# Modulation chunks of the second layer computed on VectorE instead of TensorE, in a four-layer transformer block on one Trainium2 core

## The chip, the cores and the metric

The kernel is one program on one core of a Trainium2 chip. The core has five instruction queues that matter here: TensorE (PE, with its weight loads shown as PEld), VectorE (DVE), ScalarE (ACT), GpSimd (POOL) and SyncE (SP), which issues the large loads from HBM. Every queue runs its instructions in the order in which they stand, and waits on semaphores for the others. The metric is device time of one execution in microseconds, the median over several runs.

## The reference, cut to what matters

The model has two "first" layers (a mixer and a convolutional feed-forward each) and then two more blocks. There are 256 context tokens and 256 latent tokens of width 1024. Each first layer has six modulation vectors per stream, which scale, shift and gate the activations:

```python
for l in range(DEPTH):                                   # DEPTH = 2
    mod_l = jnp.split((jax.nn.silu(c) @ ada_w[l] + ada_b[l])[:, None, :], 6, axis=-1)
    mod_c = jnp.split((jax.nn.silu(c_ctx) @ ada_w[l] + ada_b[l])[None, None, :], 6, axis=-1)
    hl = modulate(x_lat, norm_g[l, 0], mod_l[0], mod_l[1])    # rms_norm(x, g) * (1 + scale) + shift
    ...
    x_lat = x_lat + mod_l[2] * (mix_l @ w_out[l])
    x_lat = x_lat + mod_l[5] * conv_ffn(modulate(x_lat, norm_g[l, 1], mod_l[3], mod_l[4]), ...)
```

`ada_w[l]` is 1024 by 6144 in float32 (24 MB a layer), and it is multiplied by only two vectors, `silu(c)` and `silu(c_ctx)`. The feed-forward is `(silu(gate) * val) @ w_down`, where gate and val come from `h @ w_up` (1024 by 5632) through a depthwise convolution of width 3.

## The kernel before, in words

**Split products.** Activations and weights are float32. Each is split into a high part (rounded to the matmul's type) and a low part (the rest), and a product is three matmuls: high·high, high·low, low·high (`mm_t`, L438 to L445). A weight tile of 1 MB is loaded into a buffer `raw` (L390), ScalarE writes the high half (`whi`, L400) and the low half is a subtraction: on VectorE (`wlo`, L404), or on GpSimd (L402) where `pool_lo` says so. `pool_lo` is 0 except in the second feed-forward, where it is 2 (every second half). One weight tile is split as two halves of 128x1024, so it has two `whi` and two `wlo`. There are two `raw` buffers, and split halves for three to four tiles.

**The plan.** `_plan` (L126 to L228) writes down the order of all weight tiles. Modulation chunks ("ada", 256 columns of `ada_w` each, 24 a layer) are spread between them, one behind a weight tile. `w()` (L417) hands the next weight tile to a matmul stage, loads and splits one tile ahead, and on its way runs `ada()` (L535 to L560) for each chunk that it meets: 8 small products of 32 stationary columns (each shows as two matmuls in the trace, L538), a copy to SBUF (L541), two transposes (L545) and two or three VectorE instructions of 4 columns (L547 to L553). Layer 0's chunks come early; of layer 1's 24, 16 stand in the first feed-forward, one at its end, six around the second mixer and one in the second feed-forward.

**The first feed-forward** (`_ffn` with l = 0, L1267 to L1353; about 340 to 727 us of the span) runs on all 512 tokens. It goes through the hidden width in six parts (`FPARTS`): up(0), up(1), down(0), up(2), down(1), and so on; an up part has 4 weight tiles (gate and val by turns; the last part 2), a down part 2. An up tile gives two PSUM tiles of 128x512. ScalarE starts the convolution of each from PSUM (L1285), VectorE adds the two other taps from PSUM (L1288, L1289); for a val tile VectorE then multiplies by the gate (L1298, L1299) and makes a low half of the result (L645 in `hilo`). A down tile gives four PSUM tiles, each added to the residual `xt` by two VectorE instructions (L1330). PSUM tiles rotate over five banks (three tagged g, two tagged s) while `K.wide` is set. The second feed-forward runs on the 256 latent tokens alone.

**What sets the order.** The program is recorded in the order in which the Python code runs, and a scheduler then lays each engine's queue from it, with its own estimates. `_Pipe.tick` (L274) is called after every PSUM tile with the number of columns multiplied, and paces work that is interleaved with the matmuls.

Of the kernel before, what the change touches and what calls it, by code (L numbers as in the profile page):

```python
# [10 lines left out]
F32 = mybir.dt.float32  # L11
F32R = mybir.dt.float32r
BF16 = mybir.dt.bfloat16
AF = mybir.ActivationFunctionType
ALU = mybir.AluOpType
# [11 lines left out]
FPARTS = ((0, 4), (4, 4), (8, 4), (12, 4), (16, 4), (20, 2))  # L27

C_ADAB = 0
C_NG = C_ADAB + 96  # L30
# [33 lines left out]
T_MB0 = 5440  # L64
T_MB1 = 5568
T_N = 5824

PERM = [16 * c + 4 * b + a for a in range(4) for b in range(4) for c in range(16)]

# [56 lines left out]
def _plan():  # L126
    p = []
# [7 lines left out]
    def adas(l, js):  # L135
        return [(l, j, c) for j in js for c in range(4)]
# [24 lines left out]
    def spread(extra, start, tail=0, skip=0):  # L161
        q = list(extra)
        body = p[start:]
        del p[start:]
        for i, x in enumerate(body):
            p.append(x)
            if i >= skip and len(q) > tail:
                ada(*q.pop(0))
        while q:
            ada(*q.pop(0))  # L170
# [9 lines left out]
    n = len(p)  # L180
# [3 lines left out]
    n = len(p)  # L184
# [4 lines left out]
    a3, a5 = adas(0, (3,)), adas(0, (5,))  # L189
    spread(a3 + a5[:2], n, 1)  # L190
    n = len(p)
    late = adas(1, (2, 4, 3, 5))
    ffn(0)
    spread(a5[2:] + adas(1, (1, 0)) + late[:9], n, 1)
    o = ("odd_w_in", 0)
    n = len(p)
    for c0 in (512, 0, 256, 1280, 768, 1792, 1536, 1024, 2048):
        cols(o, c0, at=W_N)
    wout(1, 0)
    wout(1, 1)  # L200
    spread(late[9:16 - 1], n, 1, 3)
    n = len(p)
    ffn(1)
    spread(late[16 - 1:], n)
    a = ("a_w_in_2", 0)
    for hg in range(4):
        for g in range(3):
# [29 lines left out]
class _Pipe:  # L237
    def __init__(self):
        self.pending, self.live = [], []
        self.pace = 1e9  # L240
        self.credit = 0.0
        self.later = []

    def defer(self, cost, fn):
        self.later.append([cost, fn])
# [26 lines left out]
            self.live.append(u)  # L272

    def tick(self, cost):  # L274
        if not self.pending and not self.live:
            return
        self.credit += cost
        if self.credit >= self.pace:
            self.credit = min(self.credit - self.pace, self.pace)
            self.slot()  # L280
# [29 lines left out]
class _K:  # L310
# [221 lines left out]
    def ada(self, kind, raw, now=False):  # L532
        nc = self.nc
        _, l, j, c = kind
        acc = self.po(128, 256) if now else self.pg(128, 256)  # L535
        for k in range(KD):
            g = 32 * (k % 4)
            nc.tensor.matmul(acc[g:g + 32], self.sc[:, k, :], raw[:, k], start=(k < 4), stop=(k >= 4))  # L538
        self.pipe.tick(2048)
        sb = self.e(256)  # L540
        nc.scalar.copy(sb, acc)  # L541
        def fin():
            tp = self.pt(128, 2, 128)
            for q in range(2):
                nc.tensor.transpose(tp[:, q], sb[:, 128 * q:128 * q + 128], self.ident)  # L545
            red = self.small([128, 2, 2], "adr")
            nc.vector.tensor_reduce(red, tp.rearrange("p q (g m) -> p q m g", g=4)[:, :, 0:2, :], axis=AX.X, op=ALU.add)  # L547
            o = self.mod[l][:, j, :, 2 * c:2 * c + 2].rearrange("p t q -> p q t")
            a0 = C_ADAB + 48 * l + 8 * j + 2 * c
            nc.vector.tensor_tensor(o, red, self.cols[:, a0:a0 + 2].unsqueeze(2).to_broadcast([128, 2, 2]), op=ALU.add)  # L550
            if j in (1, 4):
                g = C_NG + 16 * l + 8 * (j // 3) + 2 * c
                nc.vector.scalar_tensor_tensor(o, o, 1.0, self.cols[:, g:g + 2].unsqueeze(2).to_broadcast([128, 2, 2]),  # L553
                                               op0=ALU.add, op1=ALU.mult)

        if now:
            fin()
        else:
            self.pipe.defer(6000, fin)

    def stat(self, n):
        return [self.sa.tile([128, n], F32, tag=f"st{n}", name=self.nm("st")), n, 0]
# [704 lines left out]
def _ffn(K, l, segs, st, nxt=None):  # L1267
    nc, tc, cols = K.nc, K.tc, K.cols
    t0, n = segs[0][0], segs[-1][1] - segs[0][0]
    ns = n // 256  # L1270
    with tc.tile_pool(name=f"f{l}", bufs=1, reuse_waits="tile") as pool, tc.tile_pool(name=f"fw{l}", bufs=3, reuse_waits="tile") as wx:
# [30 lines left out]
        def up(i):  # L1302
            f0, fn = FPARTS[i]
            G = pool.tile([128, 2, 4, n], F32R, tag="G", name=K.nm("G"), bufs=2)
            parts[i] = (G[:, 0], G[:, 1])
            for s in range(fn // 2):
                gates = {}

                def eg(m, g):
                    f = f0 + 2 * s + m  # L1310
                    gates[m] = conv(g, cw[:, 0, f:f + 1], cw[:, 1, f:f + 1], cw[:, 2, f:f + 1], cb[:, f:f + 1])

                def ev(m, g):
                    f = f0 + 2 * s + m
                    val = conv(g, hw[:, 0, f:f + 1], hw[:, 1, f:f + 1], hw[:, 2, f:f + 1], hw[:, 3, f:f + 1])
                    glu(f, G[:, 0], G[:, 1], 2 * s + m, gates[m], val)

                first = ((256, 512), (0, 256)) if split and i == 0 and s == 0 else None
                K.gemm_t(K.w(), H, n, eg, 0, first)
                K.gemm_t(K.w(), H, n, ev)  # L1320
# [17 lines left out]
                         K.norm(st[0], l + 1, 0, segs[1], 256, 3) if st else ())  # L1338

        K.wide = True  # L1340
        for i in range(len(FPARTS)):
            up(i)
            if i:
                down(i - 1)
        K.lookahead = 0
        K.wide = False
        nst = nxt(segs) if nxt else None
# [596 lines left out]
def _layout(i):  # L1944
# [28 lines left out]
            w[n, :, 1024 * x:1024 * x + 1024] = src.reshape(ka, 128, cb).transpose(1, 0, 2).reshape(128, 1024)  # L1973
    out["w"] = w
    out["tab"] = _tables()
    return out


# [15 lines left out]
```

## Time and profile before

| what | value |
|---|---|
| median of 3 runs | 1645.6 us (1642.94 to 1646.18) |
| the profiled execution, its own time | 1649.18 us |
| its span, first to last instruction | 1647.4 us |
| mean granted TensorE clock | 0.983 |
| PE busy | 1571.7 us, 95% of the span, 11390 instructions |
| PEld busy | 1378.6 us, 84% |
| DVE busy | 1118.4 us, 68%, 2168 instructions |
| ACT busy | 778.2 us, 47% |
| POOL busy | 265.2 us, 16% |
| HBM read | 228.79 MB, 140 GB/s over the span |

Shares are means over stages of different kinds; the stretch of the first feed-forward has to be read by itself. A busy PE is not PE at its peak, since matmuls overlap: the pitch from one start to the next is what counts. On VectorE an instruction also overlaps the next by a little, so again the start-to-start time is the price.

### The profile page before, as it was taken

The page shows a single profiled execution, that of the slowest core. Times are in us where ns is not written, and L with a number is a line of the kernel's source. Part 1 is how long each engine was busy: PE and PEld are TensorE (multiplying, and loading weights), DVE is VectorE, ACT ScalarE, POOL GpSimd, SP SyncE. Part 2 cuts the span into 40 slices and gives each one's busy share as a digit, 9 for nine tenths or more (in the row PEclk, how much of TensorE's full clock was granted, in tenths as well). Part 3 has the DMA queues.
Part 4 walks back from the last instruction along what each step waited for, and adds up shares of the span by engine and source line. Part 5 has one row for each costly group of instructions (what it writes and reads, how often), then busy time and mean ns, then how long its engine had stood idle before and what let it go on. Part 6 is the DMA issues. An engine that isn't in the chain of part 4 may idle for free.

```text
span 1647.4 us, 28309 instructions
## 1 busy us (share of the span) xinstructions
PE 1571.7 (95%) x11390; PEld 1378.6 (84%) x11390; DVE 1118.4 (68%) x2168; ACT 778.2 (47%) x1427; POOL 265.2 (16%) x239
## 2 busy tenths in 40 slices
PE   5999979999999999999999989999999999999998
PEld 3787857777777788888888889999989999989888
DVE  4676546675645666577677688677675767678897
ACT  3445464354323334334555555554555555555554
POOL 2221100030000000014231344441010101020111
PEclk9989989999999999998999999999999999999999
DMA  8232243334454532331333355554524343516232
GB/s 356 91 112 94 85 150 103 128 144 163 157 185 169 177 130 102 103 108 52 115 116 129 140 199 188 191 186 151 190 98 163 105 174 105 177 59 219 103 118 88
DMA packets 45107, 231.74 MB, mean 141 GB/s; under 512 B 12740, under 2 KB 15940, under 8 KB 18224
## 3 DMA queue, kind: packets, MB, share of 16 engines
q1 hardware_dynamic: 43776, 227.76, 39.9%
q10 hardware_dynamic: 1200, 2.17, 0.4%
q8 instruction: 90, 1.47, 0.4%
q14 instruction: 41, 0.34, 0.1%
HBM read 228.79 MB, written 1.12 MB: 140 GB/s over the span
## 4 chain that ended last, share of the span: by engine, by line
PE 75%; DVE 9%; ACT 4%; DMA 4%; POOL 3%; issue 2%; POOLq 0%; ACTq 0%; DVEq 0%; SPq 0%
PE g L443 10%; PE g L444 10%; PE g L445 9%; PE g L488 6%; PE g L490 6%; PE g L489 6%; PE s L443 4%; PE s L445 4%; PE s L444 4%; DMA raw<-in_w_dram 3%; DVE wlo L404 3%; PE o L1045 3%; PE t L1035 2%; PE g L538 2%; ACT whi L400 1%
## 5 line engine op out<-in xcount | busy, mean ns | idle before, releaser
L404 DVE TENSOR_TENSOR wlo<-raw,whi 128x1024 fp32r<-128x1024 f32 x289 | 358.5, 1252 | 185.8 <-ACT whi L400 185.2
L400 ACT CAST whi<-raw 128x1024 fp32r<-128x1024 f32 x322 | 332.7, 1048 | 315.2 <-DMA raw<-in_w_dram 122.9
L488 PE MATMUL g<-whi,H 128*128 128x256 f32 x1040 | 301.6, 290 | 5.5 <-ACT H L641 2.9
L490 PE MATMUL g<-whi,H 128*128 128x256 f32 x1040 | 297.3, 286 | 1.8 <-DVE H L636 1.0
L489 PE MATMUL g<-wlo,H 128*128 128x256 f32 x1040 | 296.0, 285 | 0.0
L443 PE MATMUL g<-H,whi 128*128 128x256 f32 (+1 forms) x872 | 274.5, 319 | 5.9 <-ACT H L1642 2.9
L444 PE MATMUL g<-H,whi 128*128 128x256 f32 (+1 forms) x872 | 273.7, 315 | 0.9 <-DVE H L636 0.3
L445 PE MATMUL g<-H,wlo 128*128 128x256 f32 (+1 forms) x872 | 271.7, 313 | 0.0
L488 PEld LDWEIGHTS g<-whi,H 128*128 128x128 f32 x1040 | 200.4, 193 | 13.0 <-issue 4.6
L490 PEld LDWEIGHTS g<-whi,H 128*128 128x128 f32 x1040 | 199.8, 192 | 4.0 <-DVE H L636 2.2
L489 PEld LDWEIGHTS g<-wlo,H 128*128 128x128 f32 x1040 | 200.3, 193 | 0.6 <-issue 0.2
L443 PEld LDWEIGHTS g<-H,whi 128*128 128x128 f32 x872 | 164.5, 190 | 22.4 <-ACT H L1642 3.5
L444 PEld LDWEIGHTS g<-H,whi 128*128 128x128 f32 x872 | 165.7, 190 | 13.7 <-DVE H L636 1.9
L445 PEld LDWEIGHTS g<-H,wlo 128*128 128x128 f32 x872 | 165.6, 190 | 9.5
L1009 POOL TENSOR_SCALAR P<-P,rc 128x512 f32<-128x512 f32 (+2 forms) x64 | 55.2, 863 | 491.3 <-DVE rc L1804 258.8
L402 POOL TENSOR_TENSOR wlo<-raw,whi 128x1024 fp32r<-128x1024 f32 x33 | 81.3, 2463 | 105.1 <-ACT whi L400 100.4
L445 PE MATMUL s<-H,wlo 128*128 128x256 f32 (+1 forms) x264 | 88.2, 334 | 1.9 <-DVE wlo L404 1.9
L443 PE MATMUL s<-H,whi 128*128 128x256 f32 (+1 forms) x264 | 89.2, 338 | 0.0
L444 PE MATMUL s<-H,whi 128*128 128x256 f32 (+1 forms) x264 | 87.9, 333 | 0.0
L443 PE MATMUL g<-G,whi 128*128 128x256 f32 (+1 forms) x240 | 79.2, 330 | 2.1 <-DVE e L1289 2.1
L445 PE MATMUL g<-G,wlo 128*128 128x256 f32 (+1 forms) x240 | 78.3, 326 | 0.0
L444 PE MATMUL g<-G,whi 128*128 128x256 f32 (+1 forms) x240 | 78.2, 326 | 0.0
(419 smaller groups left out, 3042.1 us busy)
## 6 DMA issues: line engine op xcount, KB each, us to landing
raw<-in_w_dram SPq DMA_DIRECT2D x209, 1024.0 KB, 4.9
xt<-in_xt_dram SPq DMA_DIRECT2D x4, 512.0 KB, 5.2
mrow<-Md ACTq DMA_DIRECT2D x8, 256.0 KB, 4.6
nab<-in_rpb_dram SPq DMA_DIRECT2D x16, 128.0 KB, 3.6
out_dram<-xt SPq DMA_DIRECT2D x4, 256.0 KB, 4.6
agw<-in_agw_dram SPq DMA_DIRECT2D x1, 512.0 KB, 13.5
mka<-in_tab_dram SPq DMA_DIRECT2D x1, 512.0 KB, 3.4
plr<-in_p_dram SPq DMA_DIRECT2D x2, 256.0 KB, 3.6
```

The source lines that it names most:

```text
L400: nc.scalar.copy(hi, raw)
L402: nc.gpsimd.tensor_tensor(lo, raw, hi.bitcast(F32), op=ALU.subtract)
L404: nc.vector.tensor_sub(lo, raw, hi.bitcast(F32))
L443: nc.tensor.matmul(out, hi[:, k, s], X[0][:, x], start=f, stop=False)
L444: nc.tensor.matmul(out, hi[:, k, s], X[1][:, x], start=False, stop=False)
L445: nc.tensor.matmul(out, lo[:, k, s], X[0][:, x], start=False, stop=l)
L488: nc.tensor.matmul(out, X[0][:, a + k, s], hi[:, k], start=f, stop=False)
L489: nc.tensor.matmul(out, X[0][:, a + k, s], lo[:, k], start=False, stop=False)
L490: nc.tensor.matmul(out, X[1][:, a + k, s], hi[:, k], start=False, stop=l)
L538: nc.tensor.matmul(acc[g:g + 32], self.sc[:, k, :], raw[:, k], start=(k < 4), stop=(k >= 4))
L1009: nc.gpsimd.tensor_scalar(P[1], P[1], rc[:, 1:2], 0.0, op0=ALU.mult, op1=ALU.add)
L1045: nc.tensor.matmul(o[64 * e:64 * e + 64], vv(e, b), u["T"][e][:, b], start=(b == 0), stop=(b == kb - 1))
```

## The change

Layer 1's 24 modulation chunks leave the plan and TensorE. A new generator `vector_ada` loads the same columns, transposed, as 48 tiles `ar` of 128x1024 (an input `v`, 512 KB each, three buffers), and loads both conditioning vectors to all partitions once (`cb`, 1 MB). VectorE then makes, for each of the 48 tiles and the two vectors, one multiply-and-sum over 1024 elements that starts from the bias and writes one column of `mod[1]`: 96 instructions, each with a read of its accumulator behind it. The first of a pair writes its products to a scratch tile `prod`, the second into `ar` itself. The generator is advanced by `tick`, one product per 8600 columns multiplied, during the first feed-forward only. In that stage `pool_lo` becomes 1 for the parts 1 to 4: GpSimd makes all low weight halves of 24 tiles, 48 subtractions that VectorE made before.

```diff
+VECTOR = [(1, j, c) for j in (1, 0, 2, 4, 3, 5) for c in range(4)]
+VPACE = 8600
...
-    late = adas(1, (2, 4, 3, 5))
     ffn(0)
-    spread(a5[2:] + adas(1, (1, 0)) + late[:9], n, 1)
+    spread(a5[2:], n)
...
-    spread(late[9:16 - 1], n, 1, 3)
-    n = len(p)
     ffn(1)
-    spread(late[16 - 1:], n)
...
     def tick(self, cost):
+        if self.side:
+            self.side(cost)
...
+    def vector_ada(self, pool):
+
+        nc = self.nc
+        cb = pool.tile([128, 2, 1024], F32, name="cb")
+        nc.sync.dma_start(cb.rearrange("p t k -> p (t k)"), self.aps["cb"].partition_broadcast(128))
+        jobs = [(l, j, 2 * c + q, n, q) for n, (l, j, c) in enumerate(VECTOR) for q in range(2)]
+
+        def fetch(i):
+            t = pool.tile([128, 1024], F32, tag="ar", name=self.nm("ar"), bufs=3)
+            nc.sync.dma_start(t, self.aps["v"][jobs[i][3]][:, 1024 * jobs[i][4]:1024 * jobs[i][4] + 1024])
+            return t
+
+        tiles = [fetch(0), fetch(1)]
+        yield
+        for t in range(2):
+            for s in (slice(0, 512), slice(512, 1024)):
+                sg = self.e(512)
+                nc.scalar.activation(sg, cb[:, t, s], AF.Tanh, scale=0.5)
+                nc.vector.tensor_scalar(sg, sg, 0.5, 0.5, op0=ALU.mult, op1=ALU.add)
+                nc.vector.tensor_mul(cb[:, t, s], cb[:, t, s], sg)
+            yield
+        for i, (l, j, m, _, _) in enumerate(jobs):
+            raw = tiles.pop(0)
+            if i + 2 < len(jobs):
+                tiles.append(fetch(i + 2))
+            a0 = C_ADAB + 48 * l + 8 * j + m
+            out = self.mod[l][:, j, :, m:m + 1]
+            for t in range(2):
+                prod = raw if t else pool.tile([128, 1024], F32, tag="prod", name=self.nm("prod"), bufs=1)
+                nc.vector.tensor_tensor_reduce(prod, raw, cb[:, t], 1.0, self.cols[:, a0:a0 + 1], ALU.mult, ALU.add,
+                                               out[:, t])
+                if t and j in (1, 4):
+                    g = C_NG + 16 * l + 8 * (j // 3) + m
+                    nc.vector.tensor_scalar(out, out, 1.0, self.cols[:, g:g + 1], op0=ALU.add, op1=ALU.mult)
+                yield
+
+    def side_step(self, steps):
+        state = [0.0]
+
+        def step(cost):
+            state[0] += cost
+            if state[0] >= VPACE:
+                state[0] -= VPACE
+                next(steps, None)
+
+        return step
...
         K.wide = True
+        steps = None
+        if split:
+            steps = K.vector_ada(pool)
+            next(steps)
+            K.pipe.side = K.side_step(steps)
         for i in range(len(FPARTS)):
+            if split:
+                K.pool_lo = int(0 < i < len(FPARTS) - 1)
             up(i)
             if i:
                 down(i - 1)
+        K.pipe.side = None
+        for _ in steps or ():
+            pass
```

**VectorE's queue, from the second weight tile of down(0) to the first tap of up(2).** In the rows, `xt_87` with L1330 (L1379 after the change) is the residual add, `adr` and `mod1` the tail of a modulation chunk, `wlo` a low weight half, and e with L1288 (L1337 after) the first tap. Before:

```order
L1330 SCALAR_TENSOR_TENSOR xt_87<-g_808_4426,mod0_105,xt_87 128x256
L547 TENSOR_REDUCE adr_810_4442<-t_809_4439 128x4
L1330 SCALAR_TENSOR_TENSOR xt_87<-g_811_4447,mod0_105,xt_87 128x256 x2
L404 TENSOR_TENSOR wlo_817_4496<-raw_815_4493,whi_816_4495 128x1024
L404 TENSOR_TENSOR wlo_819_4500<-raw_815_4493,whi_818_4499 128x1024
L1330 SCALAR_TENSOR_TENSOR xt_87<-g_812_4462,mod0_105,xt_87 128x256 x2
L1330 SCALAR_TENSOR_TENSOR xt_87<-s_813_4477,mod0_105,xt_87 128x256 x2
L547 TENSOR_REDUCE adr_826_4533<-t_825_4530 128x4
L404 TENSOR_TENSOR wlo_831_4583<-raw_829_4580,whi_830_4582 128x1024
L404 TENSOR_TENSOR wlo_833_4587<-raw_829_4580,whi_832_4586 128x1024
L1288 SCALAR_TENSOR_TENSOR e_827_4560<-g_823_4516,cols_85,e_827_4560 128x2x255
```

After, from the third PSUM tile of the same weight tile on (behind each product stands the read of its accumulator, left out here):

```order
L1379 SCALAR_TENSOR_TENSOR xt_87<-g_813_4427,mod0_105,xt_87 128x256 x2
L592 ISA ar_853_4695,mod1_106<-ar_853_4695,cb_3543,cols_85 128x1024
L1379 SCALAR_TENSOR_TENSOR xt_87<-g_814_4443,mod0_105,xt_87 128x256 x2
L592 ISA prod_880_4862,mod1_106<-ar_862_4736,cb_3543,cols_85 128x1024
L592 ISA ar_862_4736,mod1_106<-ar_862_4736,cb_3543,cols_85 128x1024
L592 ISA prod_890_4922,mod1_106<-ar_874_4810,cb_3543,cols_85 128x1024
L592 ISA ar_874_4810,mod1_106<-ar_874_4810,cb_3543,cols_85 128x1024
L592 ISA prod_901_4979,mod1_106<-ar_879_4860,cb_3543,cols_85 128x1024
L592 ISA ar_879_4860,mod1_106<-ar_879_4860,cb_3543,cols_85 128x1024
L592 ISA prod_905_5016,mod1_106<-ar_889_4920,cb_3543,cols_85 128x1024
L1337 SCALAR_TENSOR_TENSOR e_825_4512<-g_823_4473,cols_85,e_825_4512 128x2x255
```

The low halves have gone from this queue, and products stand in their place, seven in a row ahead of the first tap of up(2). They are not evenly laid: all 96 stand between up(0) and the last tile of up(3), 81 of them from the first tap of up(1) to there, and 31 in the six weight tiles of up(2) and down(1).

**SP's queue around the same place.** Each row is a load that SP issues; `raw` is a weight tile of 1 MB, or a modulation chunk of the same size. Before:

```order
L390 DMA raw_800_4403<-in_w_dram 128x2048
L390 DMA raw_807_4424<-in_w_dram 128x2048
L390 DMA raw_815_4493<-in_w_dram 128x2048
L390 DMA raw_822_4514<-in_w_dram 128x2048
L390 DMA raw_829_4580<-in_w_dram 128x2048
```

After:

```order
L392 DMA raw_829_4536<-in_w_dram 128x2048
L572 DMA ar_836_4573<-in_v_dram 128x1024
L572 DMA ar_849_4646<-in_v_dram 128x1024
L392 DMA raw_842_4622<-in_w_dram 128x2048
L572 DMA ar_853_4695<-in_v_dram 128x1024
L572 DMA ar_862_4736<-in_v_dram 128x1024
L392 DMA raw_855_4699<-in_w_dram 128x2048
L572 DMA ar_874_4810<-in_v_dram 128x1024
L572 DMA ar_879_4860<-in_v_dram 128x1024
L572 DMA ar_889_4920<-in_v_dram 128x1024
L572 DMA ar_900_4977<-in_v_dram 128x1024
L392 DMA raw_868_4785<-in_w_dram 128x2048
```

Between two weight tiles now stand two to four loads of `ar`, each of which waits until VectorE is through with the `ar` tile three earlier; a weight tile's load waits until GpSimd has made the low halves of the tile two earlier.

## Rows read from the trace of the kernel before

**Rows 1.** Busy us (count) by stretch: PE, PEld, DVE, ACT, POOL; clock; DMA share; GB/s
```profile
355.00:727.00 372.00, 371.98 (x1872) 296.61 (x1871) 227.73 (x361) 132.67 (x182) 0.28 (x1) 1.00 0.41 141
...
640.00:680.00 40.00, 40.00 (x178) 33.10 (x178) 24.57 (x37) 12.35 (x15) 0.00 (x0) 1.00 0.31 105
```
**Rows 2.** Timeline of PE around one chunk: start, us, engine, line, operation, tiles
```profile
403.43 0.39 PE L445 MATMUL s<-H,wlo 128*128 128x512 f32 x1
403.75 1.07 PE L538 MATMUL g<-raw,sc 128*32 128x256 f32 x16
404.75 0.50 PE L443 MATMUL g<-H,whi 128*128 128x512 f32 x1
...
407.41 0.39 PE L445 MATMUL g<-H,wlo 128*128 128x512 f32 x1
407.65 0.38 PE L545 MATMUL t<-ident,e 128*128 128x128 f32 x2
407.78 0.48 PE L443 MATMUL g<-H,whi 128*128 128x512 f32 x1
```
**Rows 3.** Busy time by stretch of line L538 alone: PE, PEld, clock
```profile
355.00:727.00 372.00, 18.20 (x272) 7.09 (x272) 1.00 0.41 141
727.00:925.00 198.00, 8.11 (x113) 3.05 (x113) 0.96 0.33 111
```
**Rows 4.** Timeline of PE where the second mixer begins
```profile
735.34 0.58 PE L488 MATMUL g<-whi,H 128*128 128x256 f32 x1 [2.58 <-ACT H L634]
```
**Rows 5.** Timeline of VectorE in the first feed-forward
```profile
599.22 0.88 DVE L1330 SCALAR_TENSOR_TENSOR xt<-g,mod,xt 128x256 f32<-128x256 f32 x2 [1.45 <-PE g L445]
...
630.61 0.68 DVE L1298 SCALAR_TENSOR_TENSOR e<-e,e 128x512 f32<-128x512 f32 x1
631.21 0.74 DVE L1289 SCALAR_TENSOR_TENSOR e<-g,hw,e 128x510 f32<-128x510 f32 x1
...
632.71 1.23 DVE L404 TENSOR_TENSOR wlo<-raw,whi 128x1024 fp32r<-128x1024 f32 x1
633.86 0.74 DVE L1288 SCALAR_TENSOR_TENSOR e<-s,hw,e 128x510 f32<-128x510 f32 x1
```
**Rows 6.** Timeline of VectorE in the third block: an operation with a sum
```profile
1199.18 0.69 DVE L1801 CUSTOM_DVE_ANT_0 e<-s,mka 128x512 f32<-128x512 f32 x1
...
1199.79 0.69 DVE L1664 TENSOR_TENSOR e<-g,ptcq 128x512 f32<-128x512 f32 x1
```
**Rows 7.** Groups in 1000 to 1110 us, second feed-forward: count, busy us, mean ns
```profile
L402 POOL TENSOR_TENSOR wlo<-raw,whi 128x1024 fp32r<-128x1024 f32 x20 | 48.9, 2447 | 63.2 <-ACT whi L400 58.5 <-PE s L444 4.7
...
L404 DVE TENSOR_TENSOR wlo<-raw,whi 128x1024 fp32r<-128x1024 f32 x20 | 26.2, 1311 | 23.4 <-ACT whi L400 23.4
L645 DVE TENSOR_TENSOR G<-e,G 128x256 fp32r<-128x256 f32 x12 | 13.8, 1148 | 0.0
```
**Rows 8.** Timelines of GpSimd and VectorE in the second feed-forward
```profile
1009.61 2.42 POOL L402 TENSOR_TENSOR wlo<-raw,whi 128x1024 fp32r<-128x1024 f32 x1 [3.24 <-ACT whi L400]
...
1010.02 0.48 DVE L1288 SCALAR_TENSOR_TENSOR e<-s,hw,e 128x255 f32<-128x255 f32 x1 [0.53 <-ACT e L1285]
1010.42 1.89 DVE L645 TENSOR_TENSOR G<-e,G 128x256 fp32r<-128x256 f32 x1
...
1014.55 0.42 DVE L645 TENSOR_TENSOR G<-e,G 128x256 fp32r<-128x256 f32 x1
```
**Rows 9.** Timelines of GpSimd and VectorE in the second mixer
```profile
860.31 1.94 POOL L1009 TENSOR_SCALAR P<-P,rc 128x512 f32<-128x512 f32 x1 [0.58 <-DVE rc L996]
...
867.53 0.69 POOL L1009 TENSOR_SCALAR P<-P,rc 128x512 f32<-128x512 f32 x1 [5.28 <-DVE qms L920]
...
860.15 0.49 DVE L1008 TENSOR_SCALAR P<-P,rc 128x512 f32<-128x512 f32 x1
860.55 1.22 DVE L404 TENSOR_TENSOR wlo<-raw,whi 128x1024 fp32r<-128x1024 f32 x1
```
**Rows 10.** Loads: operation, count, KB each, median us from issue to landing
```profile
raw<-in_w_dram SPq DMA_DIRECT2D x209, 1024.0 KB, 4.9
```

More of the change, by code (lines that the diff above doesn't have):

```diff
@@ L242, in __init__ @@
         self.later = []
+        self.side = None
     def defer(self, cost, fn):
@@ L1975, in _layout @@
     out["tab"] = _tables()
+    out["cb"] = np.concatenate([i["c"][0], i["c_ctx"]])
+    out["v"] = np.stack([i["ada_w"][l][:, 1024 * j + 256 * c:1024 * j + 256 * c + 256].T.reshape(2, 128, 1024)
+                         .transpose(1, 0, 2).reshape(128, 2048) for l, j, c in VECTOR])
     return out
```

## The prediction, made before the run

> **What bounds the kernel now.** I read the busy time by stretch first. In the first feed-forward TensorE is busy for 371.98 of 372 us, VectorE for 227.73, ScalarE for 132.67, and GpSimd does nothing [rows 1]. So TensorE sets the time there, and whatever leaves its queue leaves the stage, as long as nobody else becomes later than it. The second line of the group is the same stage without modulation chunks: 178 matmuls in 40 us, a pitch of 0.225 us, so a weight tile of 48 matmuls takes 10.8 us. That is the clock against which the other engines have to be held.
>
> Then the timeline around one chunk [rows 2]. From the last matmul before it to the first after it are 404.75 - 403.43 = 1.32 us instead of 0.225, and around its two transposes 407.78 - 407.41 = 0.37. A chunk costs TensorE 1.10 + 0.15 = 1.25 us; the matmuls just behind each of the two are a little late too, so I take 1.35.
>
> **What the change removes.** Line L538 alone shows 272 matmuls between 355 and 727 us, 17 chunks of 16 matmuls, and 7 chunks between 727 and 925 us [rows 3]. The plan says that one of the 17 is layer 0's and stays, and that an eighth chunk of layer 1 follows after 925 us. In the first feed-forward 16 chunks go: 16 x 1.35 = 22 us, all of it on the path, since TensorE has no gap there. Behind it 8 go, at most 8 x 1.35 = 11 us. The first of them stands where TensorE waits 2.58 us for the normalised input anyway [rows 4], and the last at the same place of the second feed-forward; I count the other six: 8 us. TensorE's saving is 30 us. The copies, transposes' consumers and 24 loads that go with the chunks lie beside it and count as nothing.
>
> **What it adds to VectorE.** The trace has no product over 1024 elements with a sum. Its two nearest rows: a subtraction of 1024 elements starts 1.15 us before the next instruction [rows 5], and the operation with a sum over 512 elements starts 0.61 us before the next, the read of its accumulator included [rows 6]; a second 512 elements cost the difference between 1.15 and 0.60 (632.71 to 633.86 against 630.61 to 631.21 [rows 5]). Both ways give 1.15 to 1.16 us; 96 products are 110 us. The 48 low halves that go to GpSimd take 48 x 1.15 = 55 us off VectorE. Spread over the whole stage this would fit (228 + 110 - 55 = 283 of some 350 us), but the new order does not spread it. So I make the sum where the products stand thickest, the 18 weight tiles of up(1) to down(2): TensorE needs 18 x 10.8 = 194 us. VectorE has there:
> - 81 products, 81 x 1.15 = 93 us;
> - 48 convolution taps of 0.74 = 35.5 us;
> - 36 gate, val and low-half operations of 0.60 = 21.5 us;
> - 48 residual adds of 0.44 (two in 0.88) = 21 us [rows 5].
>
> Together 171 us, 88% of TensorE's 194. Alone that would hold.
>
> **What GpSimd's halves do to it.** The second feed-forward already has GpSimd halves, 2.45 us each (48.9 us for 20), and there VectorE's operations on two SBUF tiles are long: 1148 ns for an L645 of 256 columns, 1311 for L404 [rows 7]. The timeline shows how: GpSimd's half runs from 1009.61 to 1012.03; the tap that reads PSUM at 1010.02 takes its usual 0.48; the L645 at 1010.42, two SBUF inputs, ends at 1012.31 after 1.89, where it takes 0.42 elsewhere [rows 8]. It stood still until GpSimd was done. The product reads `ar` and `cb`, both in SBUF. No row shows whether it is held like L645; being of the same kind of operands, I take it that it is. The Trainium skill, SBUF — State Buffer, section Who interferes with whom, says the same as a rule: a VectorE instruction with two SBUF inputs contends with a GpSimd instruction that reads SBUF, and the later one waits for the whole of the other. By it the sum is the one below; by a product that is not held it would be the first rival. The trace agrees for the two forms shown, and no run here shows the product.
>
> What a half costs VectorE has two ends. In 1000 to 1110 us the surplus is 12 x (1.15 - 0.42) + 20 x (1.31 - 1.23) = 10.4 us for 20 halves, 0.5 us each [rows 7, 8]; there VectorE had idle time for a half to fall into. The other end is the whole 2.45 us. It cannot choose its moment freely either: where a GpSimd operation (0.69 us when free) came at 860.31, it lost to VectorE's 860.15 and, straight behind it, to the L404 at 860.55, and ended at 862.25 [rows 9]. So in a row of products a half waits, and starts where VectorE turns to an operation that reads PSUM. Such runs last about 0.9 us here: the taps and adds of six tiles (16 x 0.74 + 16 x 0.44 = 19 us) fall into some 20 runs by the order. What is left of 2.45 us, 1.5, is VectorE standing still. With VectorE at 88% by itself this is nearer to the case than 0.5.
>
> 36 halves belong to the 18 tiles: 36 x 1.5 = 54 us, and VectorE needs 171 + 54 = 225 us for TensorE's 194. Five PSUM tiles let TensorE run ahead of the evacuation by about one weight tile, 10 us, which is not lost, since VectorE has no products after down(2) and can catch up there. TensorE then waits 225 - 194 - 10 = 21 us.
>
> **Queues.** SP now issues 48 loads of 512 KB and `cb` in place of the chunks' 24. A weight tile behind an `ar` is no danger, as the order asks for it three to four tiles before its use, over 30 us. The other way round there is a cost: an `ar` behind a weight tile's load waits with it for GpSimd and then for its landing, 4.9 us [rows 10], and a product that waits holds up the evacuations behind it on VectorE. In such a gap a half runs free, which gives back 1.5 us of each. I put it at zero, with up to 2 or 3 us at each of some six places in the range. GpSimd's own queue holds nothing else in the stage and would be busy for 36 x 2.45 = 88 of 194 us, so weights are late only if halves wait long. ScalarE's four activations and `cb`'s load lie at the start, beside two split tiles in stock: nothing.
>
> **The sum.** -30 + 21 = -9 us. The profiled execution took 1649.18 us, 0.2% above the median of 1645.6; 9 us from the first are 1640, and carried over to the median 1636 to 1637. I say **1636**. What the runs can tell from no change is 0.2%, 3.3 us.
>
> **Rivals.**
> - *Nothing is given back.* The products aren't held, or the halves find gaps as in the second feed-forward: 171 + 36 x 0.5 = 189 us, under 194. The whole saving stays: 1616. For it: 0.5 us was measured. Against: VectorE was busy for far less there. Chance 0.22.
> - *VectorE becomes the bound and takes more than TensorE saves.* The halves find no run to fall into, and hold VectorE 2.0 us each (the whole 2.45 less half a run): 171 + 72 = 243, less 204, gives 39 us of waiting: -30 + 39 = +9, 1655; with six gaps for `ar` of 2 us, 1667. It decides from 1.75 us a half on (171 + 63 = 234 = 204 + 30). For it: seven products stand in a row, and VectorE is full, so that any lateness stays. Against: the order does have a run of taps or adds every two or three products. Chance 0.27.
> - *A draw*, the same mechanism at 1.65 to 1.85 us a half: 1642 to 1649. Chance 0.13.
>
> The forecast has 0.38, with its own range from 1.2 us a half and 0 waiting for loads (171 + 43 - 204 = 10, so 1626) to 1.65 (1641).
>
> **The range** has to take in both sides: from 1614 (the first rival, and 2 us more of the late chunks) to 1660 (into the second rival, which has a tail above it). Faster by over 0.2%: first rival and forecast, 0.60. Within: 0.13. Slower: 0.27.
>
> **What would show it.** In the profile after, the first feed-forward must have no L538 beyond two chunks; if VectorE gives back what I think, TensorE shows idle time there of some 20 us, ended by VectorE's taps or adds, between up(2) and down(2), none in up(4) and later. The product's mean must be well above 1.2 us, with single ones near 3.5, and those must lie under a GpSimd half. The halves themselves should last up to a product longer than 2.45 us. I am wrong if products and halves overlap, if TensorE waits on weight halves instead, if gaps on VectorE end on `ar` loads, or if the second mixer gets longer.

## The result, and the profile after

The changed kernel takes **1670.65 us** (1669.61 to 1676.52, four runs), the kernel before 1644.27 us beside it: a ratio of **1.0168**, 95% interval 1.0149 to 1.0187. It is slower by 26 us, where 1636 and a gain of 9 us had been forecast. The profiled execution, at 1676.52 us the longest of the four, has a span of 1674.5 us against 1647.4. The page of the changed kernel: busy times, and the chain of waits by engine.

```profile
PE 1556.5 (93%) x10958; PEld 1375.7 (82%) x10958; DVE 1236.1 (74%) x2280; ACT 771.6 (46%) x1407; POOL 399.0 (24%) x287
...
PE 58%; DVE 25%; ACT 4%; POOL 4%; DMA 3%; issue 2%; POOLq 0%; ACTq 0%; SPq 0%; DVEq 0%
...
L592 DVE CUSTOM_DVE_ANT_0 ar<-ar,cb,cols 128x1024 f32<-128x1024 f32 x48 | 85.6, 1784 | 0.5
L592 DVE CUSTOM_DVE_ANT_0 prod<-ar,cb,cols 128x1024 f32<-128x1024 f32 x48 | 83.3, 1736 | 0.0
```

TensorE is busy for 15 us less and the span is 27 us longer, so it stands still for 42 us more. L592 is the product.

To see where, the first feed-forward is cut by VectorE's taps. The 44 PSUM tiles of the up parts each have two taps; the first tap opens the stage, the last one of tile 8 ends up(0), that of tile 32 ends up(3), and the last residual add ends the stage. Start times from the timelines, differences in us:

| stretch | before | after | change |
|---|---|---|---|
| span's start to the first tap | 357.2 | 358.5 | +1.3 |
| up(0), to the last tap of tile 8 | 36.9 | 49.4 | +12.5 |
| 16 weight tiles, to the last tap of tile 32 | 197.5 | 228.2 | +30.7 |
| to the last residual add | 140.2 | 133.8 | -6.4 |
| rest of the program | 915.6 | 904.6 | -11.0 |
| sum | 1647.4 | 1674.5 | +27.1 |

Busy time in the three middle stretches, the kernel before (columns as in [rows 1]: start and end, length, then PE, PEld, DVE, ACT and POOL, granted clock, DMA share, GB/s):

```profile
357.20:394.10 36.90, 36.90 (x199) 28.20 (x198) 24.99 (x38) 16.12 (x24) 0.00 (x0) 1.00 0.44 147
394.10:591.60 197.50, 197.50 (x1032) 153.04 (x1031) 118.58 (x191) 73.34 (x99) 0.00 (x0) 1.00 0.51 175
```

and the changed kernel:

```profile
358.50:407.90 49.40, 44.47 (x192) 34.79 (x191) 45.84 (x65) 18.83 (x25) 12.56 (x4) 0.90 0.57 198
407.90:636.10 228.20, 193.43 (x771) 153.53 (x770) 227.67 (x299) 64.39 (x82) 92.09 (x34) 0.92 0.47 167
636.10:770.40 134.30, 133.69 (x637) 112.23 (x635) 76.43 (x134) 44.12 (x61) 27.01 (x12) 1.00 0.30 96
```

In the long stretch VectorE is busy for 227.67 of 228.20 us: it is the bound now, and its work sets the length. TensorE, which had no gap there before, waits, and its mean granted clock falls to 0.92. What it waits for (waits of TensorE, 408 to 636 us: total, times, longest):

```profile
PE g L445 <- DVE e L1338: 18.3, 8, 5.3
PE s L445 <- DVE e L1338: 8.2, 4, 2.3
PE s L445 <- DVE mod L596: 5.2, 1, 5.2
PE s L445 <- DVE xt L1379: 3.1, 2, 2.4
```

These are 34.8 us, all for PSUM tiles that VectorE has not emptied (L1338 is a tap, L1379 the residual add, L596 the two-column scaling behind a product; the wait put down to it ends at 549.49 us, just behind a tap that runs from 548.60 to 549.34, and is that tap's). Why VectorE needs 228 us is seen in its timeline, in three places:

```profile
408.56 3.36 DVE L592 CUSTOM_DVE_ANT_0 ar<-ar,cb,cols 128x1024 f32<-128x1024 f32 x1
...
411.85 2.87 DVE L1348 TENSOR_TENSOR e<-e,e 128x512 f32<-128x512 f32 x1
...
414.77 1.27 DVE L592 CUSTOM_DVE_ANT_0 prod<-ar,cb,cols 128x1024 f32<-128x1024 f32 x1
...
425.91 2.38 DVE L596 TENSOR_SCALAR mod<-mod,cols 128x2 f32<-128x2 f32 x1
...
466.99 0.74 DVE L1338 SCALAR_TENSOR_TENSOR e<-s,hw,e 128x510 f32<-128x510 f32 x1
467.65 0.47 DVE L1379 SCALAR_TENSOR_TENSOR xt<-s,mod,xt 128x256 f32<-128x256 f32 x1
468.04 1.81 DVE L1348 TENSOR_TENSOR e<-e,e 128x512 f32<-128x512 f32 x1
```

GpSimd's timeline at the same times:

```profile
408.44 5.73 POOL L404 TENSOR_TENSOR wlo<-raw,whi 128x1024 fp32r<-128x1024 f32 x2 [4.26 <-ACT whi L402]
...
425.86 2.40 POOL L404 TENSOR_TENSOR wlo<-raw,whi 128x1024 fp32r<-128x1024 f32 x1 [2.41 <-ACT whi L402]
...
466.89 2.42 POOL L404 TENSOR_TENSOR wlo<-raw,whi 128x1024 fp32r<-128x1024 f32 x1 [10.24 <-ACT whi L402]
```

A product that starts just behind a GpSimd half lasts 3.36 us instead of 1.27, the gate operation L1348 under the next half 2.87 instead of 0.68, and even a scaling of two columns 2.38 instead of 0.22. Each gets through only when the half is done. The first row of GpSimd is two halves, 408.44 to 410.84 and 410.80 to 414.17; the product ends at 411.92 and the gate operation at 414.72, most of their own time behind them, and the scaling ends with its half. The half that begins at 466.89 ends at 469.31, the gate operation of 468.04 at 469.85. The tap at 466.99 and the add at 467.65, which read PSUM, run under that same half and take their usual 0.74 and 0.47 us; no tap in the 16 tiles lasts over 0.75.

### The profile page after: what moved, and what is told of

Same layout as the page of the kernel before. It is cut to its first block, busy times and chain, and to the rows that moved or that the text cites. A ratio compares the mean times of both kernels' runs of the same rounds, so it can differ in the third digit from the quotient of the medians.

```text
span 1674.5 us, 27678 instructions
## 1 busy us (share of the span) xinstructions
PE 1556.5 (93%) x10958; PEld 1375.7 (82%) x10958; DVE 1236.1 (74%) x2280; ACT 771.6 (46%) x1407; POOL 399.0 (24%) x287
## 4 chain that ended last, share of the span: by engine, by line
PE 58%; DVE 25%; ACT 4%; POOL 4%; DMA 3%; issue 2%; POOLq 0%; ACTq 0%; SPq 0%; DVEq 0%
PE g L445 7%; PE g L446 7%; PE g L447 7%; PE g L490 6%; PE g L492 5%; PE g L491 5%; DVE ar L592 5%; DVE prod L592 5%; DMA raw<-in_w_dram 3%; DVE wlo L406 3%; PE o L1094 3%; PE s L445 2%; PE s L447 2%; PE s L446 2%; PE t L1084 2%
## 5 line engine op out<-in xcount | busy, mean ns | idle before, releaser
L406 DVE TENSOR_TENSOR wlo<-raw,whi 128x1024 fp32r<-128x1024 f32 x241 | 301.6, 1260 | 133.5 <-ACT whi L402 133.1
L404 POOL TENSOR_TENSOR wlo<-raw,whi 128x1024 fp32r<-128x1024 f32 x81 | 211.4, 2614 | 314.1 <-ACT whi L402 290.1
L445 PE MATMUL g<-H,whi 128*128 128x256 f32 (+1 forms) x840 | 262.4, 316 | 11.3 <-ACT H L1701 2.7
L446 PE MATMUL g<-H,whi 128*128 128x256 f32 (+1 forms) x840 | 262.9, 314 | 1.1 <-DVE H L1703 0.4
L447 PE MATMUL g<-H,wlo 128*128 128x256 f32 (+1 forms) x840 | 260.9, 312 | 0.0
L445 PEld LDWEIGHTS g<-H,whi 128*128 128x128 f32 x840 | 157.9, 189 | 25.8 <-issue 5.2
L446 PEld LDWEIGHTS g<-H,whi 128*128 128x128 f32 x840 | 159.0, 190 | 13.4 <-DVE H L685 1.5
L445 PE MATMUL s<-H,whi 128*128 128x256 f32 (+1 forms) x296 | 101.7, 345 | 10.6 <-DVE e L1338 3.8
L446 PE MATMUL s<-H,whi 128*128 128x256 f32 (+1 forms) x296 | 101.2, 342 | 2.0 <-DVE H L685 2.0
L447 PE MATMUL s<-H,wlo 128*128 128x256 f32 (+1 forms) x296 | 101.1, 342 | 0.0
L445 PE MATMUL g<-G,whi 128*128 128x256 f32 (+1 forms) x248 | 83.6, 337 | 15.8 <-DVE e L1338 15.8
L592 DVE CUSTOM_DVE_ANT_0 ar<-ar,cb,cols 128x1024 f32<-128x1024 f32 x48 | 85.6, 1784 | 0.5
L592 DVE CUSTOM_DVE_ANT_0 prod<-ar,cb,cols 128x1024 f32<-128x1024 f32 x48 | 83.3, 1736 | 0.0
```

The source lines that it names most:

```text
L404: nc.gpsimd.tensor_tensor(lo, raw, hi.bitcast(F32), op=ALU.subtract)
L406: nc.vector.tensor_sub(lo, raw, hi.bitcast(F32))
L445: nc.tensor.matmul(out, hi[:, k, s], X[0][:, x], start=f, stop=False)
L446: nc.tensor.matmul(out, hi[:, k, s], X[1][:, x], start=False, stop=False)
L447: nc.tensor.matmul(out, lo[:, k, s], X[0][:, x], start=False, stop=l)
L592: nc.vector.tensor_tensor_reduce(prod, raw, cb[:, t], 1.0, self.cols[:, a0:a0 + 1], ALU.mult, ALU.add, out[:, t])
```

## The experiments

Ten kernels, each beside the kernel before on the same chip (medians 1644.25, 1645.47 and 1643.76 us for the three groups). The stretches are cut as in the table above.

| kernel | us | ratio to before, 95% interval | up(0) | 16 tiles | to last add |
|---|---|---|---|---|---|
| no products | 1614.06 | 0.9815 (0.9788 to 0.9843) | 42.1 | 171.6 | 139.7 |
| halves on VectorE | 1614.4 | 0.9813 (0.9786 to 0.9839) | 42.6 | 174.2 | 139.6 |
| program order, GpSimd halves | 1661.32 | 1.0096 (1.0071 to 1.0121) | 53.6 | 193.8 | 153.8 |
| program order, halves on VectorE | 1642.84 | 0.9987 (0.997 to 1.0005) | 52.7 | 178.3 | 151.0 |
| dense order, halves on ScalarE | 1619.32 | 0.9849 (0.9824 to 0.9875) | 43.3 | 175.4 | 139.1 |
| before, halves on GpSimd | 1662.21 | 1.0108 (1.0079 to 1.0136) | 37.3 | 220.9 | 134.6 |
| **halves on VectorE, `ar` loads on GpSimd's queue** | **1609.87** | **0.9786 (0.9762 to 0.981)** | 34.0 | 174.8 | 139.6 |
| every second half on GpSimd | 1638.73 | 0.9969 (0.9948 to 0.999) | 43.4 | 200.9 | 133.8 |
| one-input sums | 1621.43 | 0.9871 (0.9844 to 0.9897) | 43.1 | 172.8 | 139.7 |
| GpSimd writes only | 1614.73 | 0.9827 (0.9793 to 0.9861) | 41.2 | 176.0 | 139.4 |

**1. No products.**

```diff
-                nc.vector.tensor_tensor_reduce(prod, raw, cb[:, t], 1.0, self.cols[:, a0:a0 + 1], ALU.mult, ALU.add,
-                                               out[:, t])
...
+                if i == 0 and t == 0:
+                    nc.vector.memset(self.mod[1], 0.5)
```

> Leaves out the 96 products and the 16 scalings behind them, so the second layer's modulation is a constant 0.5; the loads of ar and cb, the GpSimd halves and the missing TensorE chunks stay. Theory A (VectorE, filled by products and held by GpSimd's halves, is the bound of the first feed-forward; TensorE's saving of 30 us is real): 1611 to 1620 us, no wait of TensorE for VectorE's taps. Rival B (the saving is smaller, or the halves and the loads delay the weights by themselves): over 1630 us. Theory C (in the first up part, weight tiles stand behind ar loads on SyncE's queue, which wait for a product): the 4.9 us of waiting for whi at 367 to 375 us are gone, since ar loads wait for nothing here; if they stay, the loads' bandwidth alone makes them.

1614.06 us. TensorE's saving is real, and neither the loads nor the GpSimd halves take it back by themselves: rival B falls. TensorE waits for no tap. Its waits for `whi` in up(0) shrink to one of 1.0 us; theory C had them gone.

**2. The low halves back on VectorE, products as they are.**

```diff
-                K.pool_lo = int(0 < i < len(FPARTS) - 1)
+                K.pool_lo = 0
```

> The changed kernel with all low halves of the first feed-forward on VectorE. The scheduler then also lays the products further apart: 52 in place of 85 between the last tap of up(0) and the last of up(3). Theory A: VectorE needs there 52 x 1.21 + 35 x 1.14 + 24 x 1.32 + 36 x 0.60 + 32 x 0.39 = 169 us for TensorE's 16 x 10.8 = 173, no holds: 1615 to 1630 us. Rival D (the products as such overfill VectorE, and GpSimd's halves are a relief): VectorE has 40 us more of its own work, 1670 us or more.

1614.4 us: 56 us faster than the changed kernel, as fast as without products, though VectorE has 48 more subtractions to make. Rival D falls. VectorE in the 16 tiles (windows, this kernel): 171 us of work for 174.

```profile
394.60:568.80 174.20, 174.20 (x771) 144.23 (x770) 171.12 (x267) 65.17 (x81) 0.00 (x0) 1.00 0.52 182
```

This run changes two things, since the scheduler also spreads the products (52 in place of 85 there). Runs 3 to 5 separate them.

**3 and 4. VectorE's queue in program order, with and without GpSimd halves.**

```diff
+        with tc.manual_schedule(engines={mybir.EngineType.DVE}) if split else nullcontext():
         for i in range(len(FPARTS)):
...
-                K.pool_lo = int(0 < i < len(FPARTS) - 1)
+                K.pool_lo = 0
```

(The second edit in run 4 only; the loop is indented under the first.)

> The changed kernel with VectorE's queue of the first feed-forward in the order in which the program is written: about three products per weight tile over the whole stage instead of five over 16 tiles; the GpSimd halves stay. Theory A: from the last tap of up(0) to the last tap of up(5) VectorE needs 74 x 1.21 + 36 x 1.32 + 54 x 0.60 + 64 x 0.39 = 194 us and 46 holds of 1.46 = 67, 261 us for TensorE's 26 x 10.8 = 281: 1615 to 1640 us, the holds still there at 1.2 to 1.6 us a half. Rival E (a single hold of 2 us in front of a tap is enough to stop TensorE, whatever the density): 1660 to 1675 us.

> Both edits: VectorE's queue in program order, and the low halves on VectorE. Theory A: 194 + 52 x 1.14 = 253 us of VectorE for 281 of TensorE, no holds: 1612 to 1630 us, not above the even order with GpSimd halves. Rival D: slower than that one by the 50 us of VectorE's own work that comes back, in part: 1650 us or more.

1661.32 and 1642.84 us, both above what theory A expected. Two causes. Program order has a cost of its own, which I had not counted: run 4 has no holds, and loses against run 2 10 us in up(0) and 11 us behind tile 32. Its waits of TensorE, 345 to 740 us, are for residual adds and low halves that stand late in that order:

```profile
PE g L445 <- DVE xt L1379: 8.1, 5, 2.7
PE g L447 <- DVE wlo L406: 7.2, 2, 6.0
...
PE s L447 <- DVE wlo L406: 2.9, 2, 1.5
```

So the pair says something only by its difference, in which this cost cancels: GpSimd halves add 18.5 us between the medians, 24.3 between the profiled executions, and 15.5 of these in the 16 tiles, although only 45 products lie there. The holds did not thin out with the products. Groups of VectorE in that stretch of run 3:

```profile
L592 DVE CUSTOM_DVE_ANT_0 ar<-ar,cb,cols 128x1024 f32<-128x1024 f32 x23 | 46.6, 2025 | 0.2
L592 DVE CUSTOM_DVE_ANT_0 prod<-ar,cb,cols 128x1024 f32<-128x1024 f32 x22 | 40.3, 1832 | 0.0
L1347 DVE SCALAR_TENSOR_TENSOR e<-e,e 128x512 f32<-128x512 f32 x12 | 18.3, 1526 | 0.0
```

Over their free durations these three and L694, L1348 and L596 have 51 us for 35 halves, 1.5 us a half. Theory A, that spreading alone would do, is half wrong, and rival E half right: the loss is smaller than with the dense order, but there is one. Rival E's time came in, though 28 us of it, the distance from run 2 to run 4, are the cost of program order and no hold.

**5. The dense order without GpSimd.**

```diff
-            nc.gpsimd.tensor_tensor(lo, raw, hi.bitcast(F32), op=ALU.subtract)
+            if self.pool_lo == 1:
+                nc.scalar.copy(lo, raw)
+            else:
+                nc.gpsimd.tensor_tensor(lo, raw, hi.bitcast(F32), op=ALU.subtract)
```

> The changed kernel, with the 48 low halves that GpSimd makes replaced by plain copies on ScalarE (so these halves are not the remainders; the low part of the products is not the reference's). VectorE's queue stays word for word as dense as in the changed kernel (85 products between the last tap of up(0) and that of up(3)), only GpSimd falls silent; ScalarE gets 48 x 1.05 = 50 us for its 133 of some 360. Theory A (the holds are the cost): VectorE's own 175 us against TensorE's 173 and 10 of lead, 1613 to 1628 us, products all at 1.2 to 1.3 us. Rival D2 (the dense order is the cost, and the halves on VectorE were fast only because the order changed with them): 1645 us or more.

1619.32 us: the order that costs 1670.65 beside GpSimd halves costs 5 us more than the spread one without them. The windows and one group of this kernel:

```profile
400.20:575.60 175.40, 175.40 (x776) 145.24 (x775) 171.79 (x299) 97.09 (x116) 0.00 (x0) 1.00 0.62 223
```

```profile
L595 DVE CUSTOM_DVE_ANT_0 prod<-ar,cb,cols 128x1024 f32<-128x1024 f32 x48 | 61.3, 1278 | 1.0 <-DMA ar<-in_v_dram 1.0
```

All products take 1.28 us, and VectorE's own work in the 16 tiles is measured: 171.8 us. The changed kernel needs 228.2 for the same queue. The 56.4 us between them are holds, but for the 0.5 us in which VectorE idles, by 34 halves: **1.66 us a half**. The operations themselves say the same: over their free durations (1.28, 0.68 and 0.22 us) the products in the changed kernel's 16 tiles are 41 us longer in sum, the gate operations and low halves of G 9, the scalings 7. Rival D2 falls.

**6. GpSimd halves in the kernel before.** The `pool_lo` line of the change, put into the kernel before.

> The kernel before, and in its first feed-forward alone the 48 low halves of parts 1 to 4 on GpSimd; no products, all chunks on TensorE. Theory A: VectorE loses 55 us of halves and gets at most 48 x 1.46 = 70 of holds in a stage in which it idles 144 us: 1640 to 1652 us, no change that can be told. Rival F (GpSimd's 2.4 us halves make weights late or hold taps at the wrong moment by themselves): 1655 us or more.

1662.21 us, 17 us slower: theory A is wrong here, and rival F right in a way. VectorE is idle for 135 of 221 us in the 16 tiles, and the surplus of its gate operations over the stage is 13 us for 50 halves, 0.3 each. TensorE's waits (394 to 615 us) name something else:

```profile
PE t L545 <- ACT e L541: 7.2, 5, 1.7
PE g L445 <- POOL wlo L402: 5.6, 6, 1.7
PE s L445 <- POOL wlo L402: 1.2, 2, 0.7
```

It waits for weight halves and for the copy behind a chunk. These waits are 14 of the 23 us by which the 16 tiles are longer. With chunks in the plan a weight tile and a chunk share the two `raw` buffers, and SyncE's loads wait 168 us in all for GpSimd's halves (345 to 700 us); but in the kernel before they wait 192 us (345 to 730 us) for VectorE's, so this sum does not show the buffers to be the reason, and the cause stays open. In the changed kernel these waits do not arise: run 1 has the halves without the chunks, and its 16 tiles take 171.6.

**7. The loads of `ar` on GpSimd's queue, on top of run 2.**

```diff
-            nc.sync.dma_start(t, self.aps["v"][jobs[i][3]][:, 1024 * jobs[i][4]:1024 * jobs[i][4] + 1024])
+            nc.gpsimd.dma_start(t, self.aps["v"][jobs[i][3]][:, 1024 * jobs[i][4]:1024 * jobs[i][4] + 1024])
```

> The version with all low halves on VectorE (1614.4 us), and the 48 loads of ar issued by GpSimd, which is idle in this stage, in place of SyncE. Theory C: the two waits of TensorE for whi in up(0), 2.3 and 2.5 us, and the matmuls at half the pitch behind them go: 1604 to 1611 us. If the loads' bandwidth, not their place in the queue, makes those waits: 1612 to 1617, waits unchanged.

1609.87 us, the fastest kernel here, 2.1% below before. Run 2 had waits for `whi` of 2.3 and 2.5 us, ending at 363 and 368 us; this one has none from its first tap on, and TensorE is busy in every us from there (windows):

```profile
355.00:389.00 34.00, 34.00 (x164) 27.37 (x163) 32.84 (x57) 16.84 (x24) 2.19 (x4) 1.00 0.54 185
389.00:563.80 174.80, 174.80 (x773) 144.76 (x772) 169.37 (x264) 66.16 (x83) 13.23 (x25) 1.00 0.53 184
```

up(0) is 8.6 us shorter than in run 2, but its first tap comes 3 us later. The reason stands ahead of it: a weight tile's load, issued at 329.96 beside `cb` and three `ar` loads, lands after 9.06 us, VectorE makes its low half at 340.12 and the feed-forward's input `H` behind that, and TensorE waits for `H` (chain of waits, then TensorE's timeline):

```profile
329.96 9.06 DMA raw<-in_w_dram
...
340.12 1.23 DVE wlo L406
```

```profile
342.37 0.79 PE L445 MATMUL g<-H,whi 128*128 128x256 f32 x2 [2.78 <-ACT H L683]
```

So the two waits for `whi` go, and one of 2.8 us comes in their place, ahead of the stretch that the table calls up(0). From its first matmul on `H` to its first on `G` (up(0) and up(1)) TensorE takes 99.0 us, and 103.6 in run 2: that gain of 4.6 us is what reaches the time (4.5 between the medians). The two intervals overlap, so its size is not settled to better than a few us.

**8. Every second half on GpSimd.**

```diff
-                K.pool_lo = int(0 < i < len(FPARTS) - 1)
+                K.pool_lo = 2 * int(0 < i < len(FPARTS) - 1)
```

> The changed kernel with every second low half of parts 1 to 4 on GpSimd, the others on VectorE. Between the last tap of up(0) and that of up(3) the order now has 70 products and 17 halves on each engine. Theory A: 70 x 1.21 + 17 x 1.14 + 32 + 22 + 12.5 + 17 x 1.46 = 195 us of VectorE for 173 and 10 of lead; 12 us of waiting and 6 to 8 of slow clock over the version without GpSimd: 1625 to 1640 us. Rival E (any hold in front of a tap stops TensorE): 1650 us or more.

1638.73 us, where theory A put it. VectorE is full again (200.79 of 200.90 us busy in the 16 tiles) with half as many halves: half the dose. Its operations last 30 us longer there than free ones, 1.7 us for each of 17 halves, and the time is 24 us above run 2, where the changed kernel is 56 above.

**9. A sum over one input in place of the product.**

```diff
-                nc.vector.tensor_tensor_reduce(prod, raw, cb[:, t], 1.0, self.cols[:, a0:a0 + 1], ALU.mult, ALU.add,
-                                               out[:, t])
+                nc.vector.tensor_reduce(out[:, t], raw, axis=mybir.AxisListType.X, op=ALU.add)
```

> The changed kernel with each product replaced by a plain sum over the same tile ar (one input from SBUF; the multiplication by cb, the bias and so the second layer's modulation are left out). GpSimd's 48 halves stay, and the order of VectorE's queue stays dense (80 of the 96 sums between the last tap of up(0) and that of up(3)). Theory G (an instruction of VectorE with two SBUF inputs is what a GpSimd half holds): the sums take 1.1 to 1.3 us each, also under a half, and the time is 1615 to 1635 us, with holds only on the gate operations and low halves of G. Rival H (whatever VectorE does in SBUF alone is held): sums of over 3 us under a half, 1655 to 1675 us.

1621.43 us, with all 48 GpSimd halves in place. Groups of VectorE and GpSimd in the stage:

```profile
L591 DVE TENSOR_REDUCE mod<-ar 128x1 f32<-128x1024 f32 x94 | 110.2, 1204 | 0.0
...
L1345 DVE SCALAR_TENSOR_TENSOR e<-e,e 128x512 f32<-128x512 f32 x22 | 20.0, 910 | 0.0
```

```profile
L404 POOL TENSOR_TENSOR wlo<-raw,whi 128x1024 fp32r<-128x1024 f32 x48 | 116.2, 2424 | 163.8 <-ACT whi L402 159.0 <-PE g L447 4.8
```

The 96 sums last 1197 to 1214 ns, none is held, while gate operations with two SBUF inputs still are (910 against 682). A sum also writes one column where a product writes a whole tile; that the write is not the reason is seen in the taps and adds, which write SBUF and are not held either (0.74 and 0.47 us under the half of 466.89). Theory G holds.

**10. GpSimd writes, but reads nothing.**

```diff
-            nc.gpsimd.tensor_tensor(lo, raw, hi.bitcast(F32), op=ALU.subtract)
+            if self.pool_lo == 1:
+                nc.gpsimd.memset(lo.bitcast(F32), 0.0)
+                nc.gpsimd.memset(lo.bitcast(F32), 0.0)
+            else:
+                nc.gpsimd.tensor_tensor(lo, raw, hi.bitcast(F32), op=ALU.subtract)
```

> The changed kernel with each of GpSimd's 48 low halves replaced by two memsets of the same tile (the low halves are zero, so the low part of these weights is left out): GpSimd writes SBUF and reads nothing. The products and their dense order stay. Theory G2 (the hold comes from GpSimd reading SBUF): products all at 1.28 us, 1613 to 1628 us, as with the halves on ScalarE (1619.3). Rival H2 (any GpSimd instruction in SBUF holds VectorE for its length): products of 1.28 us plus most of a memset's length under each, and a time above 1619 by about half of what 96 memsets take.

1614.73 us with the dense order. Groups of VectorE and of GpSimd:

```profile
L596 DVE CUSTOM_DVE_ANT_0 ar<-ar,cb,cols 128x1024 f32<-128x1024 f32 x48 | 61.4, 1279 | 0.5
```

```profile
L405 POOL MEMSET wlo<- 128x1024 f32 x48 | 46.2, 963 | 184.5 <-PE g L451 92.5 <-PE s L451 92.0
L406 POOL MEMSET wlo<- 128x1024 f32 x48 | 45.8, 956 | 2.6
```

92 us of GpSimd memsets hold no product (1267 to 1287 ns). Theory G2 holds. Runs 9 and 10 are the two halves of the mechanism: a VectorE instruction with two SBUF inputs, against a GpSimd instruction that reads SBUF. The Trainium skill, SBUF — State Buffer, section Who interferes with whom, states both conditions; the runs agree, 1.20 us for the one and 1.28 for the other, against up to 3.46 where both are met.

## Why the prediction was wrong

**TensorE's saving: right, and undersized.** 30 us were counted. Between the kernel before and run 7 the 16 tiles shorten by 197.5 - 174.8 = 22.7 us for 14 chunks, 1.62 each where I took 1.35, and the rest of the program by 915.6 - 904.8 = 10.8 us where I counted 8. With 2.9 in up(0) and 0.6 behind tile 32 it is 37 us.

**The product's price: right.** Its pitch is 1.21 us (414.77 to 415.98) for the 1.15 taken. VectorE's own work was put at 171 us and is 171.8 in run 5, which is partly luck: the 171 are 18 weight tiles with 81 products and the adds of down(2), the 171.8 are 16 tiles with 85 products and without those adds.

**The hold: right in kind, and nearly in size by luck.** 1.5 us a half were taken, 1.66 measured. Single products of 3.4 us lie under a GpSimd half, as foretold. The reason from which the 1.5 were worked out was wrong: a half does not wait for a run of PSUM readers. The longest lasts 3.40 us, 2.4 and one VectorE instruction; it gets in behind the instruction that is running, and holds the next.

**The step that failed: "TensorE needs 18 x 10.8 = 194 us".** I set VectorE's 225 us against 18 weight tiles, up(1) to down(2). All 96 products stand ahead of the last tap of up(3), so down(2)'s two tiles come too late to cover anything: VectorE's excess must be worked off within 16 tiles, 174.8 us. And of the 10 us of lead, 5.8 came back (139.6 in run 7 against 133.8 behind tile 32). With the measured terms the same sum reads 171.8 + 56.4 - 174.8 - 5.8 = 47.6 us of lost time, not 21. Of the 26.6 us between them, 19.2 are the tiles, 4.2 the lead, 2.4 the holds and 0.8 VectorE's own work. The stretch over which a sum is taken has to end where the added work ends.

**The other step that failed: "A weight tile behind an `ar` is no danger".** The reason given was that the order asks for it three to four tiles ahead. In up(0) it is not. The chain of waits of the changed kernel there:

```profile
362.30 1.20 DVE prod L592
...
363.59 1.23 DVE ar L592
...
364.92 0.26 SPq L572
...
365.29 8.34 DMA raw<-in_w_dram
...
373.65 1.05 ACT whi L402
...
374.75 0.79 PE s L445
375.54 0.43 PE g L447
```

SyncE stands at an `ar` load (L572) until a product frees its buffer, the weight tile's load behind it is issued at 365, lands 8.34 us later beside the `ar` loads, and TensorE waits 2.3 and 2.6 us for `whi`. Then the clock: TensorE's records behind the two waits are 0.43 us apart instead of 0.23 until 380 (granted clock 0.50 from 369.9 to 380.1), 16 matmuls and 3.2 us. Of up(0)'s 15.4 us (49.4 against run 7's 34.0), 6.8 are what run 2 (42.6) does not have. They are holds, which the sum left out since it began at up(1): four halves lie in up(0), and VectorE's operations there are 7.3 us longer than free ones. The other 8.6 are the difference between run 2 and run 7, and hold the waits and the clock; 3 of them only stand ahead of run 7's first tap.

**The sum, put right.** Between the profiled executions: -37.0 (saving) + 47.6 (VectorE) + 15.4 (up(0)) + 1.3 (the stage starts later) - 0.2 (the rest, 904.6 against run 7's 904.8) = 27.1, as measured. The terms are differences between the same cuts of the kernel before, run 7 and the changed kernel, so that they add up is no evidence; the runs show the single terms. The forecast of -9 is 36 us off: 26.6 by the VectorE term, 15.4 by up(0), 1.1 by the ends, less 7 by the saving.

**The rivals.** "VectorE becomes the bound" happened, by the tile count and not by the 2.0 us a half that it named; its threshold of 1.75 us was worked out from the same 194. "Nothing is given back" is what runs 2, 5 and 10 do, at 1614 to 1619 us where it said 1616, once GpSimd does not read. Of the signs: no chunk of layer 1 is left, the idle time ends on taps and adds, and there is none in the last tiles (133.69 of 134.30). It was 35 us and not 20. One of the signs of being wrong came too: TensorE waited on weight halves, 4.9 us in up(0). No product waited for its `ar`: 0.5 us of idle time stands before all 96 (the two L592 groups above).

## What to carry to other kernels

Work handed to GpSimd is not free for VectorE: a 128x1024 subtraction took 1.14 us off VectorE's queue, and under GpSimd it cost that queue 1.66 where it was full of two-input SBUF operations, 0.3 where it was 61% idle (run 6, which became slower all the same). Price an offload by what stands in the other engine's queue at that time, not by the engine's spare time in the profile. When work is added to an engine by a scheduler, read from the order where the last of it stands, and set the sum of it against the bound engine's time up to that point alone; and look at the first weight tile that shares a queue with loads that wait for a consumer.

## What the runs showed of the hardware

- **A two-column instruction can be held for a whole half.** L596 (128x2, 0.22 us free) lasted 2.38 us under a GpSimd half (the timeline at 425.91 above). In run 10, where GpSimd only writes and the products run free, L600, the same scaling, still lasts up to 0.98 us: the seven of 16 that meet a memset all end with it (two timelines, VectorE's and GpSimd's):

```profile
473.13 0.98 DVE L600 TENSOR_SCALAR mod<-mod,cols 128x2 f32<-128x2 f32 x1
473.26 1.28 DVE L596 CUSTOM_DVE_ANT_0 ar<-ar,cb,cols 128x1024 f32<-128x1024 f32 x1
```

```profile
473.13 0.96 POOL L406 MEMSET wlo<- 128x1024 f32 x1
```

  So a TENSOR_SCALAR meets GpSimd's writes too, where the two-input product does not. Here it cost little: the product behind it starts 0.13 us later. The Trainium skill, SBUF — State Buffer, section Who interferes with whom, lists TENSOR_SCALAR among the operations that can take the shared pair of ports, if their operands meet its conditions; this row agrees.
- **TensorE ran at the lower clock behind a wait, and in a VectorE-bound stretch that need not cost anything of its own.** Behind the wait of 5.35 us (timeline of the changed kernel) twelve matmuls of 512 columns follow 0.43 us apart, 1.2 GHz (granted clock 0.58 from 463 to 470 us), and then it is back at 0.23, 2.4 GHz (1.00 from 470 to 476):

```profile
463.55 0.77 PE L445 MATMUL g<-G,whi 128*128 128x512 f32 x1 [5.35 <-DVE e L1338]
464.11 0.63 PE L446 MATMUL g<-G,whi 128*128 128x512 f32 x1
464.54 0.63 PE L447 MATMUL g<-G,wlo 128*128 128x512 f32 x1
```

  Some 70 slow matmuls lie in the long stretch, 15 us of surplus. But VectorE idles for half a us of its 228, so its work sets the length, and a faster TensorE would only have waited more; this is argued from the idle time, and no run has the stretch without the slow clock.
